# Inputs handed over with features on the partitions, and six PSUM banks for the first two column tiles

## The chip, the cores and the metric

The program runs on one core of a Trainium2 chip. The metric is the device time of one execution in microseconds (us). TensorE (PE; its weight loads are PEld), VectorE (DVE), ScalarE (ACT), GpSimd (POOL) and SyncE (SP) each run their own instructions in a fixed order; they wait for each other through semaphores. Nearly all DMAs are issued on SP's queue, and a DMA that waits holds up every DMA behind it in that queue.

## The reference

One layer of a decoder over 1024 prompt tokens and 8 sample requests of 4 tokens (1056 tokens), in float32:

```
x = x + mixer(rmsnorm(x, g_mix)) @ w_out       # retention (4 heads) and HGRN2 (4 heads), one projection w_in
x = x + cross_attn(rmsnorm(x, g_xa))           # 256 memory tokens, 4 heads of 256
x = x + swiglu(rmsnorm(x, g_ffn))
y = rmsnorm(x, g_final)
mem_k, mem_v = rmsnorm(mem, g_mem) @ w_xk, rmsnorm(mem, g_mem) @ w_xv    # prompt memory, both are outputs
rmsnorm(x, g) = x * rsqrt(mean(x*x, -1) + 1e-6) * g
```

The prompt attends to `mem_k` and `mem_v`; the sample requests attend to cached keys and values, `cache_mem_k[0, b, m, h, d]` for request b, memory token m, head h. Outputs are y, the recurrent states and the prompt's memory keys and values.

## The kernel before

**Layout.** Activations lie with features on the partitions: 8 tiles of 128 features, 1056 tokens wide, in three column blocks `GS` of 384, 384 and 288 tokens. Every float32 product is made of three matmuls (helper `mms`, line 220): both operands are split into a high part (a copy, on ACT, L195) and a low part (the difference, on POOL or DVE, L196 for weights), and high*high, high*low and low*high are summed in PSUM.

**Items.** A weight matrix is worked in column tiles of 128 features, each an `Item`. `run` takes an item: for every token block, 24 matmuls (8 feature tiles by three) into one PSUM bank, then an evacuation (`evac`). During an item the next item's weights are split (`w_split`), and at its end the weights of the item three on are loaded (`w_raw`, two DMAs of 256 KB into four `wraw` buffers). After each half of an item `tick` lets the generators in `sides` do one step each; all side work (recurrences, attention, loads) enters the instruction order that way. PSUM has eight banks: `mm` 2, `sm` 3, `o` 2, `u` 1.

**Start.** Tokens arrive with tokens on the partitions (`load_x`, nine tiles `xt`). `x_unit(g, k)` brings feature tile k of token block g to features first: PE transposes of up to three 128-token tiles (L789), ACT writes the high part scaled by the gain (L790), ACT or DVE writes the raw copy `xraw` (L792, L794), DVE the low part (L795). 24 units are worked in block order `GO` = (2, 0, 1), three units ahead of the matmuls of the first two items: the first HGRN2 head's query (item 0) and forget gate (item 1). `x_squares` (L799 on ACT, L801 on DVE) sums the squares of a token tile, `rstd_small` takes them to a power on POOL (L315), and `x_bcast` spreads the factors over the partitions with PE (L319, bank `u`) and a DVE copy into `rbc` (L809). An evacuation multiplies a bank by `rbc`, so it needs the block's factors; the two `mm` banks are used again for each block. The raw copies are stored to DRAM (`xT_d`) and come back as the residual. Gains come as rows and are transposed (L755). Item 2 (the value) follows under `run`.

**Later places.** `mem_load` brings the memory tokens in and transposes them (L913), inside the second retention head. `kv_proj_item` makes the memory keys (8 items, then 8 for the values); a side step transposes each result back to tokens first (L955), ACT copies it (L957) and SP stores it (L965). `sample_keys` loads the cached keys (`kb`, L1090), transposes them (32 steps of four, L1103) and ACT copies them to `keyT` (L1105), eight ahead of their use in `sample_attend`. These steps lie in the output projection (`c_items`, from the fifth on) and in the query projection of the cross attention.

Of the kernel before, what the change touches and what calls it, by code (L numbers as in the profile page):

```python
# [44 lines left out]
VB = 4  # L45
KLEAD = 2
PAUSES = {1: 2, 8: 2, 9: 2, 14: 0, 15: 0, 16: 0, 17: 0}
# [9 lines left out]
class Item:  # L57


    def __init__(self, src, kt, xs, evac, cols=GS, start=None, end=None, l_eng="pool", k0=0):  # L60
        self.src, self.kt, self.xs, self.evac, self.cols = src, kt, xs, evac, cols
        self.start, self.end, self.l_eng, self.k0 = start, end, l_eng, k0
        self.ks = range(kt)
        self.pieces = 2
        self.wide = False
        self.steps = None
        self.side_by_side = 3
        self.banks = None
        self.dst = None
        self.same = None  # L70
        self.split = None
        self.before_last = None

    def prepare(self, n):
# [18 lines left out]
def build(tc, ctx, a, outs):  # L93
# [29 lines left out]
    def ub():  # L123
        return psum("u", 1)
# [135 lines left out]
    def run(items):  # L260

        for it in items:
# [92 lines left out]

    xT_d = dr.tile([KT, P, T], F32, name="xT_d")
    x1_d = dr.tile([KT, P, T], F32, name="x1_d")
# [384 lines left out]

    gts = [hw.tile([n, P], F32, name="gt", tag="on", bufs=2) for n in (16, 32)]

    def load_gain(n):
        r0, r = gcol[n]
        src = a[n] if n == "hg_lb" else a[n][0:1]
        gt, r0 = (gts[0], r0) if r0 < 16 else (gts[1], r0 - 16)
        act.dma_start(gt[r0:r0 + r], src.rearrange("l (h p) -> (l h) p", p=P))

    def put_gains(i):
        n, lo = (16, 0), (32, 16)
        n, lo = (n, lo)[i]
        g_ps = ub()
        pe.transpose(g_ps[:, 0:n], gts[i], ident[:n, :n])  # L755
        dve.tensor_copy(gains[:, lo:lo + n], g_ps[:, 0:n])

    GO = (2, 0, 1)
    act.dma_start(ident, a["c_ident"])
    load_x(6)  # L760
    for n in ("g_mix", "hg_lb"):
        load_gain(n)
    load_x(7)
    load_x(8)
    w_raw()
    for i in (0, 1, 2):
        load_x(i)
    w_raw()
    for i in (3, 4, 5):
        load_x(i)  # L770
    dve.memset(ones, 1.0)
# [5 lines left out]

    xraw = [act_tile(k) for k in range(KT)]
    ss = tp.tile([P, 16], F32, name="ss", tag="ss", bufs=1)
# [3 lines left out]
    def x_unit(g, k):  # L783
        c = GS[g]
        w = width(g)
        pt = (sm if k % 2 else ob)()[:, :w]
        for i, rows in tiles_of(g):
            lo = i * P - c.start
            pe.transpose(pt[:, lo:lo + rows], xt[i][:rows, k * P:(k + 1) * P], ident[:rows, :rows])  # L789
        act.activation(X["h"][k][:, c], pt, AF.Copy, scale=gain("g_mix", k))  # L790
        if k % 2:
            act.activation(xraw[k][:, c], pt, AF.Copy)  # L792
        else:
            dve.tensor_copy(xraw[k][:, c], pt)  # L794
        dve.scalar_tensor_tensor(X["l"][k][:, c], pt, gain("g_mix", k), X["h"][k][:, c].bitcast(F32), op0=ALU.mult, op1=ALU.subtract)  # L795

# [25 lines left out]

    put_gains(0)
    xunits = [(g, k) for g in GO for k in range(KT)]
    AHEAD = 3
    for u in xunits[:AHEAD]:
        x_unit(*u)
        if u == xunits[0]:
            w_split()
    for n in ("g_xa", "g_mem", "g_ffn", "ret_gain", "hg_gain"):  # L830
        load_gain(n)
    first = mix_items[:2]
    w_first = []
    for it in first:
        it.start()
    banks = None

    def first_mms(j, g, k):
        mms(banks[j], pairs_of(first[j], w_first[j], GS[g], (k,)), first=(k == 0), last=(k == KT - 1))

    for n_, (g, k) in enumerate(xunits):
        if n_ + AHEAD < len(xunits):
            x_unit(*xunits[n_ + AHEAD])
        if k == 0:
            banks = [mm()[:, :width(g)] for _ in first]
        if n_ == 0:
            w_first.append(splits.pop(0))
        first_mms(0, g, k)
# [7 lines left out]
        if k == 5:  # L856
            x_bcast(g)
        if n_ == 2:
            lower_bound()
        if n_ == 4:  # L860
            act.activation(lw[:, 0, 0:1], ones[:, 0:1], AF.Sigmoid)
        if k == 3 and g != GO[-1]:
            for i, rows in tiles_of(GO[GO.index(g) + 1]):
                x_squares(i, rows)
        if n_ == 1:
            for i, rows in tiles_of(g):
                x_squares(i, rows)
        if n_ == KT - 1:
            put_gains(1)
        if k == KT - 1:  # L870
            first[0].evac(banks[0], g)
            if g == GO[-1]:
                w_split()
                for k_ in range(KT):
                    first_mms(1, g, k_)
            first[1].evac(banks[1], g)
        if n_ == KT:
            w_raw()
            w_raw()
            for t, n in ((lmask, "c_lmask"), (bsel, "c_bsel")):  # L880
                sp.dma_start(t, a[n])
    w_raw()
    done[0] = 2
    for k in (4, 5, 6, 7, 0, 1, 2, 3):
        sp.dma_start(xT_d[k], xraw[k])
    rope += [btile(0), btile(1)]
# [13 lines left out]
    def mem_load():  # L900
# [3 lines left out]
        mss = tp.tile([P, 4], F32, name="mss", bufs=1)  # L904
        for c in range(2):
            for i in range(2):
# [5 lines left out]
                for k in range(4):  # L912
                    pe.transpose(pt[:, k * P:(k + 1) * P], mtok[:, k * P:(k + 1) * P], ident)  # L913
                dve.tensor_copy(mT[c][:, :, i * P:(i + 1) * P], pt.rearrange("p (k t) -> p k t", k=4))
                act.activation(mtok, mtok, AF.Square, accum_out=mss[:, 2 * c + i:2 * c + i + 1])
                yield
# [26 lines left out]
    def kv_proj_item(wname, m, is_k, l_eng):  # L943
        def ev(pt, g):
            if is_k:
                t32 = k32(m)
            else:
                t32 = tmp("sg")[:, :NMEM]
            dve.tensor_tensor(t32, pt, kvs["rbm"][:, :NMEM], op=ALU.mult)

            def rest():
# [6 lines left out]
                ms = slice(m * P, (m + 1) * P)  # L958
                if not is_k:
                    for i in range(2):  # L960
                        act.activation(kvs["vh"][i][:, ms], tt[:, i * P:(i + 1) * P], AF.Copy)
                        dve.tensor_tensor(kvs["vl"][i][:, ms], tt[:, i * P:(i + 1) * P], kvs["vh"][i][:, ms].bitcast(F32), op=ALU.subtract)
                out = mk_o if is_k else mv_o
                yield
                sp.dma_start(out[0, 0].rearrange("(i p) h d -> p i (h d)", p=P)[:, :, ms], st.rearrange("p (i e) -> p i e", i=2))  # L965

# [64 lines left out]

    run(mix_items[2:4])
    for h in range(1, NH):
# [23 lines left out]
    def split_heads():  # L1057
        for i in range(6):
            yield
        for k in ORD[:6]:  # L1060
# [3 lines left out]
            yield  # L1064
            reload(k, xT_d, st_c)
            yield
# [16 lines left out]
    def sample_keys():  # L1083

        kbs = {}

        def load(n):
            if n < NH * NB:
                kbs[n] = kv.tile([P, 2, NMEM], F32, name="kb", bufs=KLEAD + 1)
                sp.dma_start(kbs[n], a["cache_mem_k"][0, n % NB, :, n // NB].rearrange("(i p) d -> p i d", p=P))  # L1090

        for n in range(KLEAD):
            load(n)
            yield
        for n in range(NH * NB):
            while kstate["made"] - kstate["used"] >= KTB:
                yield
            load(n + KLEAD)
            pt = sm()
            kb = kbs.pop(n)  # L1100
            for e_ in range(2):
                for i in range(2):
# [15 lines left out]
    nothing = lambda: None  # L1118
    c_items[0].stepwise(ORD, [nothing] * 6 + [lambda k=k: split_o(k) for k in ORD[6:]] + [lambda k=k: reload(k, xT_d, st_c) for k in ORD[6:]])
    c_items[-1].ks = ORD  # L1120
# [762 lines left out]
    for n_, (c, tiles) in enumerate(FG):  # L1883
# [22 lines left out]
        else:  # L1906
# [10 lines left out]
        'w_up', 'w_down', 'g_final']  # L1917
_OUTS = [(1, 1024, 1024), (8, 4, 1024), (1, 1, 4, 128, 128), (1, 1, 4, 128, 128), (1, 1, 256, 4, 256), (1, 1, 256, 4, 256),
         (1, 8, 4, 128, 128), (1, 8, 4, 128, 128)]
# [36 lines left out]


# [16 lines left out]
```

## Time and profile before

| | |
|---|---|
| median of 3 runs | 1737.16 us (1736.64 to 1738.53) |
| the profiled execution, its own time | 1737.18 us |
| its span, first to last instruction | 1735.4 us |
| PE busy | 1683.4 us, 97% of the span |
| DVE, ACT, POOL busy | 855.6, 567.6, 595.1 us |
| DMA moved | 154.83 MB, 89 GB/s on average |

The rows below read as follows. A timeline row gives start, duration, engine, line, operation, result and operands with their tile names, shape and count, and in brackets the idle time of the engine before it with what ended that. Successive matmuls overlap, so the distance between two starts is the time that one takes from its engine. A chain row is a piece of the chain of work that ended last. A row of a table by stretches gives the busy time of each engine in the stretch (with instruction counts), then the granted TensorE clock, the busy share of the DMA engines, and GB/s.

### The profile page before, as it was taken

What the parts mean: (1) busy time and instruction counts of PE and PEld (TensorE: products, weight loads), DVE (VectorE), ACT (ScalarE), POOL (GpSimd) and SP (SyncE); (2) the same over time, 40 slices, a digit from 0 to 9 for tenths busy, and PEclk for the clock granted to TensorE, in tenths of its full rate; (3) what the DMA queues carried; (4) which work ended last, traced back from release to release, by engine and by line L of the source; (5) the groups of instructions that cost most, each with busy time, mean ns of one, the idle gap of its engine ahead of it and who ended that gap; (6) DMA issues with size and microseconds to landing.
All of it is one profiled execution on the core that took longest, in us unless ns stands there. A gap on an engine that the chain in (4) does not pass through costs nothing.

```text
span 1735.4 us, 33455 instructions
## 1 busy us (share of the span) xinstructions
PE 1683.4 (97%) x13752; PEld 1616.6 (93%) x13752; DVE 855.6 (49%) x1625; ACT 567.6 (33%) x1162; POOL 595.1 (34%) x511
## 2 busy tenths in 40 slices
PE   7999999999999999999999889999999999999997
PEld 6999889899999899999989889999999999999987
DVE  6365565532336511422246986665565666322335
ACT  5221222232225522344444452223322223221213
POOL 2222223433543543200032235555555552222211
PEclk9999999999999999999999999999999999999999
DMA  4511211122215734133243212222222224332112
GB/s 153 181 40 50 64 38 52 41 85 62 63 31 148 232 115 158 51 122 116 92 130 87 73 31 75 75 83 93 90 75 81 75 75 138 99 101 90 59 46 101
DMA packets 206968, 154.83 MB, mean 89 GB/s; under 512 B 8784, under 2 KB 191904, under 8 KB 206816
## 3 DMA queue, kind: packets, MB, share of 16 engines
q1 hardware_dynamic: 206576, 152.61, 28.3%
q8 instruction: 108, 1.77, 0.4%
q14 instruction: 44, 0.36, 0.1%
q10 hardware_dynamic: 240, 0.09, 0.0%
HBM read 122.06 MB, written 30.61 MB: 88 GB/s over the span
## 4 chain that ended last, share of the span: by engine, by line
PE 83%; DVE 6%; issue 4%; ACT 3%; DMA 2%; POOL 2%; SPq 0%; ACTq 0%; POOLq 0%; DVEq 0%
PE mm L220 52%; PE o L220 12%; PE sm L220 7%; PE sm L1158 1%; PE sm L532 1%; PE u L422 1%; PE sm L1103 1%; PE o L435 1%; PE u L220 1%; PE sm L403 1%; PE o L437 1%; ACT wh L195 1%; POOL xl L305 1%; POOL wl L196 1%; DMA wraw<-in_w_xo_dram 1%
## 5 line engine op out<-in xcount | busy, mean ns | idle before, releaser
L220 PE MATMUL mm<-xh,wh 128*128 128x384 f32 (+3 forms) x1756 | 565.9, 329 | 5.3 <-DVE z L674 1.9
L220 PE MATMUL mm<-xl,wh 128*128 128x384 f32 (+3 forms) x1756 | 544.9, 317 | 0.8 <-DVE xl L305 0.5
L220 PE MATMUL mm<-xh,wl 128*128 128x384 f32 (+4 forms) x1692 | 537.8, 318 | 2.9 <-POOL wl L196 2.9
L196 POOL TENSOR_TENSOR wl<-wraw,wh 128x512 fp32r<-128x512 f32 (+2 forms) x155 | 191.4, 1250 | 518.3 <-ACT wh L195 399.7
L220 PEld LDWEIGHTS mm<-xh,wh 128*128 128x128 f32 x1756 | 328.1, 189 | 20.5 <-issue 14.2
L220 PEld LDWEIGHTS mm<-xl,wh 128*128 128x128 f32 x1756 | 328.5, 190 | 2.4 <-DVE xl L305 0.9
L220 PEld LDWEIGHTS mm<-xh,wl 128*128 128x128 f32 x1692 | 320.0, 189 | 4.3 <-POOL wl L196 3.8
L195 ACT ACTIVATE wh<-wraw 128x512 fp32r<-128x512 f32 (+2 forms) x266 | 153.8, 600 | 316.6 <-PE mm L220 136.1
L196 DVE TENSOR_TENSOR wl<-wraw,wh 128x512 fp32r<-128x512 f32 (+1 forms) x111 | 112.1, 1014 | 34.7 <-ACT wh L195 31.8
L220 PE MATMUL o<-xl,wh 128*128 128x264 f32 (+2 forms) x444 | 127.8, 288 | 0.2
L220 PE MATMUL o<-xh,wh 128*128 128x264 f32 (+2 forms) x444 | 127.8, 288 | 0.0
L220 PE MATMUL o<-xh,wl 128*128 128x264 f32 (+2 forms) x444 | 127.4, 287 | 0.0
L220 PE MATMUL mm<-n,wh 128*128 128x264 f32 (+2 forms) x586 | 123.9, 302 | 3.2 <-ACT n L195 1.6
L1588 POOL TENSOR_TENSOR sil<-sil,rbc 128x528 f32<-128x528 f32 x44 | 63.2, 1456 | 137.9 <-ACT sil L1587 137.9
L220 PEld LDWEIGHTS mm<-n,wh 128*128 128x128 f32 x586 | 95.5, 188 | 4.1 <-ACT n L195 1.9
L1752 DVE TENSOR_TENSOR a<-mm,a 128x384 f32<-128x384 f32 (+1 forms) x71 | 37.3, 525 | 122.7 <-PE mm L220 122.6
L195 ACT ACTIVATE wh<-sum 128x512 fp32r<-128x512 f32 x88 | 55.3, 629 | 115.3 <-PE o L220 69.0
L220 PE MATMUL mm<-n,wl 128*128 128x264 f32 (+2 forms) x293 | 88.3, 302 | 0.7 <-POOL wl L196 0.7
L220 PEld LDWEIGHTS o<-xl,wh 128*128 128x128 f32 x444 | 84.0, 189 | 0.9 <-POOL xl L305 0.8
L220 PEld LDWEIGHTS o<-xh,wh 128*128 128x128 f32 x444 | 84.0, 189 | 0.0
L220 PEld LDWEIGHTS o<-xh,wl 128*128 128x128 f32 x444 | 83.6, 188 | 0.0
L315 POOL TENSOR_TENSOR orr<-rs,nhalf 128x4 f32<-128x4 f32 (+3 forms) x33 | 27.7, 840 | 139.7 <-DVE rs L314 129.9
(450 smaller groups left out, 3147.4 us busy)
## 6 DMA issues: line engine op xcount, KB each, us to landing
wraw<-in_w_in_dram SPq DMA_DIRECT2D x64, 256.0 KB, 2.9
wraw<-in_w_gate_dram SPq DMA_DIRECT2D x44, 256.0 KB, 2.9
wraw<-in_w_up_dram SPq DMA_DIRECT2D x44, 256.0 KB, 2.9
p_d<-sil SPq DMA_DIRECT2D x40, 264.0 KB, 3.5
vb<-in_cache_mem_v_dram SPq DMA_DIRECT2D x32, 256.0 KB, 3.9
kb<-in_cache_mem_k_dram SPq DMA_DIRECT2D x32, 256.0 KB, 2.7
wraw<-in_w_down_dram SPq DMA_DIRECT2D x32, 256.0 KB, 2.8
wraw<-in_w_xo_dram SPq DMA_DIRECT2D x23, 256.0 KB, 4.1
```

The source lines that it names most:

```text
L195: act.activation(h_, src, AF.Copy)
L196: e.tensor_tensor(l_, src, h_.bitcast(F32), op=ALU.subtract)
L220: pe.matmul(out, l_, r_, start=(first and i == 0), stop=(last and i == n - 1), **kw)
L305: e.tensor_tensor(xl[:, cc], src[:, cc], xh[:, cc].bitcast(F32), op=ALU.subtract)
L315: pool.tensor_tensor(out, t[:rows, :n], nhalf[:rows, :n], op=ALU.pow)
L403: pe.transpose(pt[:, c * P:(c + 1) * P], src[:, lo:lo + P], ident)
L422: pe.matmul(u[:, c * P:(c + 1) * P], ktok[:, cc * P:(cc + 1) * P], vtok[:, cc * P:(cc + 1) * P], start=True, stop=True)
L435: pe.matmul(dst, att[:, cc * P:(cc + 1) * P], vtok[:, cc * P:(cc + 1) * P], start=True, stop=(cc == 0))
L437: pe.matmul(dst, q[:, cc * P:(cc + 1) * P], S[:, cc - 1], start=False, stop=True)
L532: pe.matmul(pt[32 * j:32 * j + 32, c * w:(c + 1) * w], kk[:, lo:lo + 32], t_, start=True, stop=True)
L1588: pool.tensor_tensor(both, both, r[:, c2_], op=ALU.mult)
L1752: dve.tensor_tensor(x2[m][:, GS[g]], pt, x2[m][:, GS[g]], op=ALU.add)
```

## The change

- The host hands over the tokens also features first (`x_T`), the gains as columns (`c_gains`), the sample's keys features first, 2 KB per partition (`cache_mem_k`), and the memory tokens features first (`c_memT`); the prompt's memory keys are written features first and turned by the host.
- `x_unit` becomes two instructions, high and low part, out of a loaded tile; its transposes, raw copy and bank are gone. Tokens in token order are still loaded, for the squares, behind `x_T` of their block. `xT_d` and its eight stores are gone; the residual is read from `x_T`.
- The first item's weights and the gains come on ACT's queue; its two low parts are both made on DVE.
- The first two items use six banks, two for each token block (`mm`, `o`, `sm`). Squares, broadcast and evacuation move back: block 2's squares to the 12th unit and its evacuation behind the 16th; block 0's squares behind both items; block 0's evacuation, block 1's squares and block 1's evacuation into `first_rest`, a side generator that runs in item 2, which takes its blocks in the order `GO`.
- The transposes of memory tokens, of memory keys (with their ACT copy) and of the sample's keys (with theirs) are gone; DMAs write `mT` and `keyT`, and the key result is stored by SP in the evacuation itself.

```diff
@@ -268,9 +268,9 @@
-                for g in range(len(it.cols)):
-                    group(it, w, g, g == 0)
-                    if g == 1:
+                for n_, g in enumerate(it.order or range(len(it.cols))):
+                    group(it, w, g, n_ == 0)
+                    if n_ == 1:
                         w_raw()
@@ -740,34 +739,27 @@
+    act.dma_start(gains, a["c_gains"])
+    first = mix_items[:2]
+    raws[0] = [wtile("wraw", KH, F32) for _ in range(2)]
+    for t, ks in zip(raws[0], halves(KT)):
+        act.dma_start(t, first[0].src[ks.start * P:ks.stop * P].rearrange("(k p) m -> p k m", p=P))
...
     act.dma_start(ident, a["c_ident"])
...
+    load_T(2, range(4))
+    load_T(2, range(4, KT))
     w_raw()
-    for i in (0, 1, 2):
+    load_T(0, range(KT))
+    for i in (6, 7, 8):
         load_x(i)
...
+    load_T(1, range(KT))
@@ -775,24 +767,14 @@
     def x_unit(g, k):
-        c = GS[g]
-        w = width(g)
-        pt = (sm if k % 2 else ob)()[:, :w]
-        for i, rows in tiles_of(g):
-            lo = i * P - c.start
-            pe.transpose(pt[:, lo:lo + rows], xt[i][:rows, k * P:(k + 1) * P], ident[:rows, :rows])
-        act.activation(X["h"][k][:, c], pt, AF.Copy, scale=gain("g_mix", k))
-        if k % 2:
-            act.activation(xraw[k][:, c], pt, AF.Copy)
-        else:
-            dve.tensor_copy(xraw[k][:, c], pt)
-        dve.scalar_tensor_tensor(X["l"][k][:, c], pt, gain("g_mix", k), X["h"][k][:, c].bitcast(F32), op0=ALU.mult, op1=ALU.subtract)
+        x, h_, l_ = (t[k][:, GS[g]] for t in (xraw, X["h"], X["l"]))
+        act.activation(h_, x, AF.Copy, scale=gain("g_mix", k))
+        dve.scalar_tensor_tensor(l_, x, gain("g_mix", k), h_.bitcast(F32), op0=ALU.mult, op1=ALU.subtract)
@@ -820,31 +802,37 @@
+    banks = {g: [f()[:, :width(g)] for _ in first] for g, f in zip(GO, (mm, ob, sm))}
...
+        if n_ == 11:
+            squares(GO[0])
+        if n_ == 15:
+            first_evac(GO[0])
+    w_split()
+    for k_ in range(KT):
+        first_mms(1, GO[-1], k_)
+    squares(GO[1])
...
+    def first_rest():
+        first_evac(GO[1])
+        squares(GO[2])
+        yield
+        first_evac(GO[2])
+
+    mix_items[2].order = GO
+    side(first_rest())
+    run(mix_items[2:3])
@@ -947,6 +932,9 @@
             dve.tensor_tensor(t32, pt, kvs["rbm"][:, :NMEM], op=ALU.mult)
+            if is_k:
+                sp.dma_start(mk_o[m], t32)
+                return
@@ -1082,27 +1068,11 @@
-            load(n + KLEAD)
-            pt = sm()
-            kb = kbs.pop(n)
-            for e_ in range(2):
-                for i in range(2):
-                    pe.transpose(pt[:, (2 * e_ + i) * P:(2 * e_ + i + 1) * P], kb[:, i, e_ * P:(e_ + 1) * P], ident)
             keyT[n] = kv.tile([P, 2, NMEM], F32, name="keyT", bufs=KTB)
-            act.activation(keyT[n], pt.rearrange("p (e m) -> p e m", e=2), AF.Copy)
+            sp.dma_start(keyT[n], a["cache_mem_k"][n // NB, n % NB])
```

How the instruction order moves, at three places.

DVE, at the end of the start, before: the squares (`s`, `ss`) of block 1 stand between the low parts (`xl`) of the last units, ahead of the broadcast copy (`rbc`) of block 0.

```order
L314 TENSOR_SCALAR rs<-ss 128x1
L801 SCALAR_TENSOR_TENSOR s_162,ss<-b_121 128x1024
L314 TENSOR_SCALAR rs<-ss 128x1 x2
L795 SCALAR_TENSOR_TENSOR xl_116<-sm,gains,xh_108 128x384
L794 COPY a_151<-o 128x384
L795 SCALAR_TENSOR_TENSOR xl_109<-o,gains,xh_101 128x384
L809 COPY rbc<-u 128x384
```

The same squares now, on DVE, in item 2: between the two last broadcast copies stand an evacuation of block 0 (items 0 and 1, out of the `o` banks) and the squares, then the value's first evacuation (`V`).

```order
L791 COPY rbc<-u 128x384
L673 TENSOR_TENSOR z<-o,rbc 128x384
L683 TENSOR_TENSOR z<-o,rbc 128x384
L685 TENSOR_SCALAR b_193<-sg,oml,lower 128x384
L686 TENSOR_SCALAR b_192<-b_193 128x384
L314 TENSOR_SCALAR rs<-ss 128x1
L783 SCALAR_TENSOR_TENSOR s_176,ss<-b_120 128x1024
L314 TENSOR_SCALAR rs<-ss 128x1 x2
L660 TENSOR_TENSOR V<-mm,rbc 128x288
L791 COPY rbc<-u 128x384
```

What moved: block 1's squares went from ahead of block 0's broadcast to behind its evacuation, and its own broadcast follows them directly. On PE the two broadcasts (L319) stand 12 matmuls of 288 columns apart.

SP, in the memory keys, before: each key store (`out_4`, out of ACT's copy `z`) and the weight loads after it.

```order
L178 DMA wraw_6110<-in_w_xk_dram 128x4x128
L178 DMA wraw_6112<-in_w_xk_dram 128x4x128
L1052 DMA a4_6160<-xT_d_91 128x1056
L965 DMA out_4_dram<-z_6165 128x2x128
L178 DMA wraw_6186<-in_w_xk_dram 128x4x128
L178 DMA wraw_6188<-in_w_xk_dram 128x4x128
```

And now:

```order
L936 DMA out_4_dram<-b0_5867 128x256
L178 DMA wraw_5966<-in_w_xk_dram 128x4x128
L178 DMA wraw_5968<-in_w_xk_dram 128x4x128
L1038 DMA a4_6016<-in_x_T_dram 128x1056
L936 DMA out_4_dram<-b0_5867 128x256
```

What moved: the store of key tile m stood behind the weight loads issued at the end of item m, and waited for a copy made inside item m+1; it now stands ahead of those loads and waits for the evacuation of item m.

PE, in the fifth tile of the output projection, before: the first of the 32 steps that transpose the sample's keys.

```order
L220 MATMUL mm_7427<-xl3_7015,wh_7291 128x384
L220 MATMUL mm_7427<-xh3_7014,wl_7292 128x384
L1103 MATMUL sm_7442<-ident_83,kb_7407 128x128 x4
L220 MATMUL mm_7427<-xh4_6086,wh_7295 128x384
L220 MATMUL mm_7427<-xl4_6087,wh_7295 128x384
```

And now:

```order
L220 MATMUL mm_7242<-xh3_6829,wh_7106 128x384
L220 MATMUL mm_7242<-xl3_6830,wh_7106 128x384
L220 MATMUL mm_7242<-xh3_6829,wl_7107 128x384
L220 MATMUL mm_7242<-xh4_5941,wh_7110 128x384
L220 MATMUL mm_7242<-xl4_5942,wh_7110 128x384
```

What moved: the four transposes are gone, as at the other 31 steps; apart from removed transposes and the start up to item 2, PE's order is the same in both kernels.

## Rows read from the trace of the kernel before

**Rows 1.** The page: PE's busy time, and the engines' shares of the chain that ended last.

```profile
PE 1683.4 (97%) x13752; PEld 1616.6 (93%) x13752; DVE 855.6 (49%) x1625; ACT 567.6 (33%) x1162; POOL 595.1 (34%) x511
...
PE 83%; DVE 6%; issue 4%; ACT 3%; DMA 2%; POOL 2%; SPq 0%; ACTq 0%; POOLq 0%; DVEq 0%
```

**Rows 2.** The instructions of line 1103, the transposes of the sample's keys: durations (ns, least, median, most), first and last start (us).

```profile
L1103 PE MATMUL sm<-ident,kb x128: 270/272/474, 655.3 to 847.3; 128*128 128x128 f32 x128
```

**Rows 3.** The chain in the output projection, where the key transposes begin (start, us, engine, tile, line).

```profile
650.18 5.02 DMA kb<-in_cache_mem_k_dram
...
655.25 1.11 PE sm L1103 x4
656.37 3.17 PE mm L220 x12
659.54 0.44 PE sm L1103 x4
...
671.64 2.10 PE mm L220 x12
```

**Rows 4.** The timeline of PE there: the first key transposes with the wait ahead of them, and two matmuls of 384 columns behind.

```profile
655.25 1.11 PE L1103 MATMUL sm<-ident,kb 128*128 128x128 f32 x4 [2.19 <-DMA kb<-in_cache_mem_k_dram]
...
656.80 0.52 PE L220 MATMUL mm<-xh,wl 128*128 128x384 f32 x1
657.12 0.52 PE L220 MATMUL mm<-xh,wh 128*128 128x384 f32 x1
```

**Rows 5.** Busy time by stretches around that place, and (last row) in the query projection of the cross attention.

```profile
654.00:656.00 2.00, 0.75 (x4) 0.75 (x5) 0.00 (x0) 0.00 (x0) 0.00 (x0) 0.79 0.70 245
656.00:658.00 2.00, 2.00 (x8) 2.00 (x7) 0.00 (x0) 0.60 (x1) 0.00 (x0) 0.50 0.22 61
...
740.00:750.00 10.00, 10.00 (x75) 8.80 (x75) 3.04 (x7) 6.35 (x17) 0.00 (x0) 1.00 0.49 153
```

**Rows 6.** The start by stretches: to the first projection matmul; to where both items have five feature tiles of block 2; to the end of items 0 and 1; to the end of item 2.

```profile
0.00:10.35 10.35, 3.62 (x13) 2.04 (x13) 2.05 (x6) 3.96 (x8) 1.48 (x5) 1.00 0.83 265
10.35:22.91 12.56, 11.98 (x44) 9.62 (x44) 11.72 (x32) 8.16 (x18) 5.12 (x5) 1.00 0.95 299
22.91:52.74 29.83, 27.98 (x182) 26.67 (x181) 22.51 (x45) 17.14 (x35) 7.86 (x10) 1.00 0.02 5
52.74:64.44 11.70, 11.70 (x74) 11.70 (x73) 2.65 (x6) 2.20 (x4) 3.44 (x3) 1.00 0.96 367
```

**Rows 7.** The timeline of PE in the start: the wait for item 1's low weights, and matmuls of 288 columns early and later.

```profile
19.62 0.61 PE L220 MATMUL mm<-xh,wl 128*128 128x288 f32 x1 [0.51 <-POOL wl L196]
...
20.50 0.44 PE L220 MATMUL mm<-xh,wl 128*128 128x288 f32 x1
20.75 0.44 PE L220 MATMUL mm<-xh,wh 128*128 128x288 f32 x1
...
24.02 0.29 PE L220 MATMUL mm<-xh,wh 128*128 128x288 f32 x1
24.16 0.29 PE L220 MATMUL mm<-xl,wh 128*128 128x288 f32 x1
```

**Rows 8.** DMA issues of the first 60 us: tile, count, size of each, median us from issue to landing.

```profile
wraw<-in_w_in_dram SPq DMA_DIRECT2D x10, 256.0 KB, 5.7
...
vtok<-in_x_prompt_dram SPq DMA_DIRECT2D x1, 512.0 KB, 4.1
```

**Rows 9.** Low parts of weights on DVE over the whole run: count, durations (ns, least, median, most).

```profile
L196 DVE TENSOR_TENSOR wl<-wraw,wh x111: 416/693/1815, 9.5 to 1467.1; 128x512 fp32r<-128x512 f32 x109, 128x256 fp32r<-128x256 f32 x2
```

**Rows 10.** The timeline of ACT, DVE and POOL in the start, for durations: a square on ACT and on DVE, three factors on POOL, a low part, the broadcast copy, a first product, a sigmoid, two high parts of weights, a gate.

```profile
12.54 1.05 ACT L799 ACTIVATE S<-ktok 128x1024 f32<-128x1024 f32 x1
13.48 1.21 DVE L801 SCALAR_TENSOR_TENSOR s<-vtok 128x1024 f32<-128x1024 f32 x1
21.60 2.61 POOL L315 TENSOR_TENSOR rr<-rs,nhalf 128x1 f32<-128x1 f32 x3 [2.03 <-DVE rs L314]
47.28 0.61 DVE L795 SCALAR_TENSOR_TENSOR xl<-sm,gains,xh 128x384 fp32r<-128x384 f32 x1
47.81 0.55 DVE L809 COPY rbc<-u 128x384 f32<-128x384 f32 x1
48.87 0.56 DVE L674 TENSOR_TENSOR z<-mm,rbc 128x384 f32<-128x384 f32 x1 [0.51 <-PE mm L220]
49.46 0.53 ACT L675 ACTIVATE sg<-z 128x384 f32<-128x384 f32 x1 [2.57 <-DVE z L674]
49.89 1.14 ACT L195 ACTIVATE wh<-wraw 128x512 fp32r<-128x512 f32 x2
54.24 0.48 DVE L686 TENSOR_SCALAR b<-sg,oml,lower 128x384 f32<-128x384 f32 x1 [0.66 <-ACT sg L685]
```

**Rows 11.** The instructions of lines 913 and 955, the transposes of memory tokens and of memory keys: durations (ns, least, median, most), first and last start (us).

```profile
L913 PE MATMUL sm<-ident,lmask x16: 272/273/273, 355.1 to 381.9; 128*128 128x128 f32 x16
...
L955 PE MATMUL sm<-ident,b x16: 271/272/328, 545.1 to 572.0; 128*128 128x128 f32 x16
```

**Rows 12.** The timeline at the end of the memory keys: SP's issue of weights, POOL's low part of the same weights, and PE's first use of that low part.

```profile
570.14 1.12 SPq L178 DMA_DIRECT2D wraw<-in_w_xv_dram  x2
...
575.61 1.30 POOL L196 TENSOR_TENSOR wl<-wraw,wh 128x512 fp32r<-128x512 f32 x1 [2.04 <-ACT wh L195]
...
576.96 0.39 PE L220 MATMUL mm<-xh,wl 128*128 128x256 f32 x1
```

More of the change, by code (lines that the diff above doesn't have):

```diff
@@ L72, in __init__ @@
         self.before_last = None
+        self.order = None
     def prepare(self, n):
@@ L821, in lower_bound, with squares, first_evac @@
         dve.tensor_scalar(oml, lower, -1.0, 1.0, op0=ALU.mult, op1=ALU.add)
-    put_gains(0)
     xunits = [(g, k) for g in GO for k in range(KT)]
     AHEAD = 3
-    for u in xunits[:AHEAD]:
-        x_unit(*u)
[L828 to L833, printed above, removed]
+    splits[0] = first[0].split = ([], [])
+    wstate["split"] = 1
+    for u, raw in zip(xunits[:2], raws.pop(0)):
+        h_, l_ = wtile("wh", KH), wtile("wl", KH)
+        split2(h_, l_, raw, dve)
+        splits[0][0].append(h_)
+        splits[0][1].append(l_)
+        x_unit(*u)
+    x_unit(*xunits[2])
+    w_first = [splits.pop(0)]
     for it in first:
         it.start()
-    banks = None
+    banks = {g: [f()[:, :width(g)] for _ in first] for g, f in zip(GO, (mm, ob, sm))}
     def first_mms(j, g, k):
-        mms(banks[j], pairs_of(first[j], w_first[j], GS[g], (k,)), first=(k == 0), last=(k == KT - 1))
+        mms(banks[g][j], pairs_of(first[j], w_first[j], GS[g], (k,)), first=(k == 0), last=(k == KT - 1))
+    def squares(g):
+        for i, rows in tiles_of(g):
+            x_squares(i, rows)
+    def first_evac(g):
+        x_bcast(g)
+        for it, bank in zip(first, banks[g]):
+            it.evac(bank, g)
     for n_, (g, k) in enumerate(xunits):
@@ L855, in build @@
                 first_mms(1, g, k_)
-        if k == 5:
-            x_bcast(g)
         if n_ == 2:
             lower_bound()
-        if n_ == 4:
+        if n_ == 6:
             act.activation(lw[:, 0, 0:1], ones[:, 0:1], AF.Sigmoid)
[L862 to L876, printed above, removed]
         if n_ == KT:
             w_raw()
+            for i in range(6):
+                load_x(i)
             w_raw()
@@ L1064, in split_heads @@
             yield
-            reload(k, xT_d, st_c)
+            reload(k, a["x_T"], st_c)
             yield
@@ L1083, in sample_keys @@
     def sample_keys():
[L1085 to L1094, printed above, removed]
         for n in range(NH * NB):
@@ L1118, in build @@
     nothing = lambda: None
-    c_items[0].stepwise(ORD, [nothing] * 6 + [lambda k=k: split_o(k) for k in ORD[6:]] + [lambda k=k: reload(k, xT_d, st_c) for k in ORD[6:]])
+    c_items[0].stepwise(ORD, [nothing] * 6 + [lambda k=k: split_o(k) for k in ORD[6:]] + [lambda k=k: reload(k, a["x_T"], st_c) for k in ORD[6:]])
     c_items[-1].ks = ORD
@@ L1955, in shape_constants, with laid_out @@
     return c
+def laid_out(inputs):
+    data = {n: np.ascontiguousarray(inputs[n]) for n in _INS if n[:2] != "g_" and n[-5:] != "_gain" or n == "g_final"}
+    keys = np.asarray(inputs["cache_mem_k"])[0].transpose(2, 0, 3, 1).reshape(NH, NB, 2, P, NMEM)
+    data["cache_mem_k"] = np.ascontiguousarray(keys.transpose(0, 1, 3, 2, 4))
+    rows = [np.asarray(inputs[n]).reshape(-1, P) for n in ("g_mix", "hg_lb", "g_xa", "g_mem", "g_ffn", "ret_gain", "hg_gain")]
+    data["c_gains"] = np.ascontiguousarray(np.pad(np.concatenate(rows).T, ((0, 0), (0, 48 - sum(len(r) for r in rows)))))
+    tokens = np.concatenate([np.asarray(inputs[n]).reshape(-1, D) for n in ("x_prompt", "x_sample")])
+    data["x_T"] = np.ascontiguousarray(tokens.T.reshape(KT, P, T))
+    data["c_memT"] = np.ascontiguousarray(np.asarray(inputs["mem_prompt"])[0].T.reshape(2, 4, P, NMEM).transpose(0, 2, 1, 3))
+    return data
 def kernel(**inputs):
@@ L1963 @@
     arrays, aps = {}, {}
-    data = {n: np.ascontiguousarray(inputs[n]) for n in _INS}
+    data = laid_out(inputs)
     data.update(shape_constants())
```

58 lines of the change are left out of this document (15 added, 43 removed).

## The prediction

> **What bounds the kernel now.** I read the page first: PE is busy 97% of the span and makes up 83% of the chain that ended last [rows 1]. So one instruction taken out of PE's order is worth its whole time wherever PE runs without a gap, and nothing where PE waits at that place anyway. Next I read the places that the change touches, one by one: the key transposes in the chain and the timeline [rows 2 to 5], the start by stretches [rows 6], where PE is busy but its matmuls stand at twice the later distance [rows 7], and last the memory tokens and keys. All sums are made against the profiled execution, 1737.18 us, which is within 0.02 us of the median.
>
> **The sample's keys: 17.6 us off.** 32 steps of four transposes go [rows 2]. A step stands in the chain with 0.44 us [rows 3], and in the query projection, where they lie densest, PE is busy 10.00 of 10 us [rows 5]: nothing hides them. 31 x 0.44 = 13.6. The first step runs from 655.25 to the next matmul, 0.8 us, at half pace. Ahead of it PE waits 2.19 us for `kb` [rows 4]; the chain shows that DMA, 5.02 us, as the releaser [rows 3]. Behind it 12 matmuls take 3.17 us where 12 later ones take 2.10 [rows 3]: the granted clock falls to 0.79 in the stretch of the wait and 0.50 in the next [rows 5], the level of 1.2 GHz, and matmuls of 384 columns stand 0.32 us apart [rows 4] instead of 2.10/12 = 0.175. That is 1.07. Sum 13.6 + 0.8 + 2.2 + 1.07 = 17.6. ACT's 32 copies go too, but ACT isn't on the path there. The new key loads need only a free `keyT`, which `sample_attend` releases eight requests ahead of use, so I cost them at nothing on PE; their cover is those eight slots, and if it fails PE waits for a load, up to the 5.02 us of [rows 3] once. Bounds: 13.5 (the wait, its slow matmuls and the half-pace part come back elsewhere) to 18.5.
>
> First what the trace shows: after 2.19 us without work PE ran at the lower level. The Trainium skill, "TensorE: Matmul & The Clock Gate", section "Why this matters for your kernels", warns of PE-idle gaps between bursts of matmuls because the clock goes back to half; by that rule the change, which takes this gap away and makes a new one in item 2 (below), gains 1.07 here and loses some 1.7 there, which is what the rows give as well.
>
> **The start, to the end of item 2: 6.3 us off (2 to 11).** Item 2 now ends at 64.44 [rows 6]. I rebuild it with the new orders.
> - First matmul. Before, the gains, nine PE transposes and the split stand ahead of it, at 10.35 [rows 6]. Now only the gains, item 0's weights and `x_T` are needed. A 512 KB load issued at 0.74 landed 4.1 us later, a weight load of 256 KB takes 5.7 in the median [rows 8]: usable at 5.0 to 7, I take 5.0, since this load is early in its queue. ACT's high part (0.57) and a DVE low part (0.69, [rows 9]) follow: first matmul about 6.1.
> - Block 2. DVE makes both weight low parts and the first units' `xl` (0.5 each) and paces PE to 8.25, five units of item 0 are done at 10.9. Item 1's weights, behind eight token loads on SP, are split at 12.05 (ACT, two in 1.14, [rows 10]) and 13.35 (POOL, 1.28 a low part). 13 matmuls at 0.24 [rows 7] end at 16.45, the point that before is reached at 22.91: 6.5 earlier. I keep the half pace, since before the 0.24 spacing lasts to about 4 us behind the last wait at 19.62 [rows 7].
> - Blocks 0 and 1 of items 0 and 1. Each unit loses three PE transposes. 4 x 0.24 + 14 x 0.133 + 48 x 0.175 give 27.65 at the end of block 0; block 2's broadcast 0.7; item 0's 24 matmuls in two parts with a wait of 1.55 between (unit 20's low part stands behind block 2's evacuation on DVE: copy 0.45, two products, two gates and the `xl`, some 0.5 each [rows 10]); item 1's 24 x 0.175. End at 38.35, before 52.74: 14.4 earlier.
> - Item 2, blocks 2 and 0. 12 x 0.133, block 0's broadcast (its factors are ready by about 39.5, no wait), 12 x 0.133: 42.2. Then PE stands before the second broadcast. Behind it is DVE's row in the order: the copy of block 0, two products, two gates, the squares; on ACT two sigmoids and two squares of 1.05 + 0.19; on POOL the factors, 2.61/3 = 0.87 each [rows 10]. From the first broadcast's end: 0.55 + 2 x 0.56 + 0.53 + 1.24 + 1.21 + 0.35 + 2 x 0.83 = 6.6, so the factors come at 47.2 and **PE idles 5.0 us**. Queued behind on PE are item 2's last 48 matmuls, which need none of these factors. Then 0.7 + 48 x 0.175 = 56.3, and as at 654 the clock should fall: there the half pace lasted from 655.25 to about 658.4 [rows 3, 4], and half of that time, 1.6, is lost; I take 1.8 for the longer wait. End 58.1 against 64.44.
>
> The tokens cost nothing in this sum. 10.2 MB of inputs (twice 4.33 MB of tokens, six weight loads of 256 KB) must land by about 42 us; the stretches of the start moved 265 to 367 GB/s where loads were queued [rows 6], which takes 38 us at the lowest rate. The bounds 2 and 11: no early start of the weights and a longer wait in item 2 (8), against no wait there.
>
> **Memory tokens: 1.75 us off.** 16 transposes in four groups of four, 4 x 0.44, in a dense stretch [rows 11]. Both bounds within 0.3.
>
> **Memory keys: 1.0 us off (-1.5 to 2.1).** 16 transposes, eight pairs [rows 11], at 0.11 each from half of an 0.44 step of four, are 1.8 to 2.1 us. What is added: SP's store of item m now waits for that item's evacuation and stands ahead of the next weight loads, where before it waited for a copy of the item before. Queued behind are the weight loads, then ACT, POOL and PE. That path is just in time: the load issued at 570.14 feeds a low part at 575.61 to 576.91, which PE uses at 576.96 [rows 12]. An evacuation's 0.56 [rows 10] and one issue of 0.5 in a few items takes back some half.
>
> **Sum.** 17.6 + 6.3 + 1.75 + 1.0 = 26.6, so 1737.18 - 26.6 = 1710.5. Gains put in as columns, the removed stores of `xT_d` and ACT's lost copies are off the path; their DMA moved beside PE at full pace.
>
> **Rivals.**
> - *A, the clock rises earlier, or does not fall at item 2's wait:* 1.8 us more, 1708.7. For it: with no transposes the early matmuls are all full ones. Against: the half pace in [rows 4] after a shorter wait. In the start the granted-clock column reads 1.00 [rows 6] although the spacing is that of the lower level [rows 7], so rows don't decide it. The Trainium skill, "TensorE: Matmul & The Clock Gate", section "Part 4: PE-mode transpose", holds that transposes don't count as PE work for the clock; by that rule the rise comes earlier here. Chance 0.12.
> - *B, weights later through the memory keys:* eight items each lose the store's wait, eight times some 0.5 instead of the gain of 1.0: 1710.5 + 4 = 1714.5. For it: the just-in-time path of [rows 12]; against: one item in view only. Chance 0.10.
> - *C, the attention's own latency takes the place of the key steps:* the steps stand between scores and probabilities of the sample attention; if 24 of the 32 only filled such waits, 24 x 0.44 = 10.5 is lost: 1721. Against: PE without any gap in [rows 5]. Chance 0.10.
> - *D, six banks don't do what they say:* the wait moves from a block's end to item 2 and is 8 us more than the 5 that I put, or the first weights come as late as before: 1718. Chance 0.08.
> - *E, slower than before:* the start becomes bound by its loads, since x is loaded twice. The rows of [rows 6] give 265 to 299 GB/s; 10.2 MB would have to come below some 140 GB/s, 73 us in place of 42, to lose more than the 27 that the rest gains. Reads of 1152 or 1536 bytes a row might be slower than token rows of 4 KB; a factor of two is unlikely. Past 1741. Chance 0.02.
>
> **How the numbers follow.** The forecast has 0.58, and A to E the chances above. The range is 1702 to 1720: it holds the forecast with its bounds (the keys' 13.5, the start's 2 to 11; all low bounds at once are unlikely), A, B and D, and leaves C and E out. A gain below 0.2%, 3.5 us, is about what a measurement of this kernel can't tell from no change; only E with a mild rate or C with D come there: same 0.03, slower 0.02, faster 0.95.
>
> **What would show it.** In the profile of the changed kernel: no line of key transposes and no wait or clock below 1.00 near 650 to 660; the query projection still without gaps (else C); items 0 and 1 ending near 38 and item 2 near 58, with one wait of about 5 us before its second broadcast and a shorter one in unit 20 of the start; first matmul near 6; in the memory keys, whether PE waits for `wl` more than before (B). If item 2 ends past 62, the start's step is wrong (D or E); if it ends before 55, the wait for block 1's factors is.

## The result: slower, where 27 us less was forecast

| | before | changed |
|---|---|---|
| median (4 runs each) | 1737.65 us (1736.64 to 1738.53) | 1757.81 us (1755.62 to 1758.81) |
| ratio to before | 1 | 1.0114, 95% interval 1.0097 to 1.0132 |
| the profiled execution, its own time | 1737.18 us | 1758.38 us |
| its span | 1735.4 us | 1756.4 us |

The changed kernel is 20 us slower; the forecast of 1710.5 us and its range of 1702 to 1720 were wrong. The page of the changed kernel answers to [rows 1]: PE is busy 6.6 us less, in a longer span; its share of the chain falls from 83% to 80%, and DMA's rises from 2% to 4%.

```profile
PE 1676.8 (95%) x13518; PEld 1605.7 (91%) x13518; DVE 841.1 (48%) x1608; ACT 545.2 (31%) x1110; POOL 593.6 (34%) x510
...
PE 80%; DVE 6%; issue 5%; DMA 4%; ACT 3%; POOL 2%; SPq 0%; POOLq 0%; ACTq 0%; DVEq 0%
```

Where the time went is read by following the first or last start of one and the same line in both traces (the view of a line):

| place | before | changed | moved since the place above |
|---|---|---|---|
| first evacuation of the item behind item 2 | 68.9 | 60.5 | -8.4 |
| first evacuation of a memory key | 542.4 | 533.5 | -0.5 |
| first evacuation of the output projection | 611.0 | 644.2 | **+42.1** |
| last evacuation of the cross attention's query | 874.6 | 889.3 | -18.5 |
| first scaled tile for the layer behind the cross attention (DVE, line 1384 before) | 936.3 | 956.0 | +5.0 |
| last instructions on the output (DVE, line 1862 before) | 1730.5 | 1751.4 | +1.2 |

So the start and the sample's keys gave what the prediction wanted of them. Sixteen items in between, the memory keys and values, lost more than both. PE's waits in the changed kernel (total us, times, longest) name it; in the kernel before, the first of these isn't in the list, and the second stands with 3.6 us:

```profile
PE mm L220 <- ACT wh L195: 15.8, 13, 3.2
PE mm L220 <- POOL wl L196: 11.8, 15, 0.9
PE mm L220 <- ACT xh L776: 6.4, 2, 6.2
PE u L319 <- POOL rr L315: 5.3, 2, 3.6
PE sm L943 <- DVE sg L934: 5.1, 7, 3.5
```

PE waits for split weights. The evacuations of memory keys (tile `b`) and values (tile `sg`), first and last start, give the time of an item: (586.0 - 533.5)/7 = 7.50 us for a key and 5.40 for a value, where the kernel before (line 949) took 4.03 and 3.63.

```profile
L949 DVE TENSOR_TENSOR b<-mm,rbc x8: 409/422/425, 542.4 to 570.6; 128x256 f32<-128x256 f32 x8
L949 DVE TENSOR_TENSOR sg<-mm,rbc x8: 411/414/414, 574.0 to 599.4; 128x256 f32<-128x256 f32 x8
...
L934 DVE TENSOR_TENSOR b<-mm,rbc x8: 409/417/424, 533.5 to 586.0; 128x256 f32<-128x256 f32 x8
L934 DVE TENSOR_TENSOR sg<-mm,rbc x8: 414/415/417, 592.4 to 630.2; 128x256 f32<-128x256 f32 x8
```

The chain that ended last, followed through one memory key, shows what an item waits for (L936 is the store of the key, L178 the load of weights). The four rows behind the chain are from the timelines of PE, DVE and SP: the last matmul of the next item, its evacuation, its store and the load behind that.

```profile
542.03 0.34 DVE b L934
...
542.38 0.36 SPq L936
...
542.79 0.43 SPq L178
...
543.26 3.36 DMA wraw<-in_w_xk_dram
...
546.73 0.64 ACT wh L195
...
547.39 1.01 DVE wl L196
548.40 0.60 DVE on L450
549.00 0.60 DVE oss L444
...
549.63 0.24 DVE rs L314
...
543.89 0.28 PE L220 MATMUL mm<-xl,wl 128*128 128x256 f32 x1
...
549.77 0.42 DVE L934 TENSOR_TENSOR b<-mm,rbc 128x256 f32<-128x256 f32 x1
...
550.21 0.36 SPq L936 DMA_DIRECT2D out_dram<-b  x1
550.68 0.97 SPq L178 DMA_DIRECT2D wraw<-in_w_xk_dram  x2
```

It is a closed loop: an evacuation releases the key store on SP; behind the store SP issues the next weights; they land, ACT and DVE split them; and DVE reaches the next evacuation (549.77) only behind that split, because `w_split` stands ahead of `evac` in the program. PE had ended the matmuls of that next item at 544.2, so its bank stood ready for 5.6 us. SP then issues the next load at 550.68, 7.9 us after the last. One item's load is in flight at a time. In [rows 12] the load issued at 570.14 had 6.8 us until PE used it, while the loads of other items went on beside it.

The stretches show what this does: the whole of the sixteen items, before and changed; one piece of them in the changed kernel, with the granted clock at 0.54; then the ten microseconds in which the first of the sample's keys are loaded (683.4), which answer to [rows 5], now without a gap.

```profile
542.40:611.00 68.60, 65.04 (x536) 62.38 (x537) 40.24 (x80) 34.68 (x72) 35.79 (x27) 1.00 0.76 225
533.50:644.20 110.70, 82.76 (x519) 73.39 (x520) 37.42 (x79) 33.91 (x66) 35.19 (x28) 0.85 0.49 145
...
560.00:570.00 10.00, 7.82 (x54) 5.66 (x55) 2.33 (x4) 3.51 (x6) 2.54 (x2) 0.54 0.50 155
...
680.00:690.00 10.00, 10.00 (x62) 10.00 (x62) 1.57 (x3) 2.54 (x5) 4.61 (x5) 1.00 0.86 289
```

The 42.1 us have two parts. PE stands idle for 27.9 us of the sixteen items (110.70 - 82.76) where it stood idle for 3.6 before, 24.4 us more; and it is busy 17.7 us longer with fewer instructions, at a granted clock of 0.85 in place of 1.00.

### The profile page after: what moved, and what is told of

Same layout as the page of the kernel before. It is cut to its first block, busy times and chain, and to the rows that moved or that the text cites. A ratio compares the mean times of both kernels' runs of the same rounds, so it can differ in the third digit from the quotient of the medians.

```text
span 1756.4 us, 32900 instructions
## 1 busy us (share of the span) xinstructions
PE 1676.8 (95%) x13518; PEld 1605.7 (91%) x13518; DVE 841.1 (48%) x1608; ACT 545.2 (31%) x1110; POOL 593.6 (34%) x510
## 3 DMA queue, kind: packets, MB, share of 16 engines
q8 instruction: 106, 1.74, 0.4%
## 4 chain that ended last, share of the span: by engine, by line
PE 80%; DVE 6%; issue 5%; DMA 4%; ACT 3%; POOL 2%; SPq 0%; POOLq 0%; ACTq 0%; DVEq 0%
PE mm L220 50%; PE o L220 12%; PE sm L220 7%; DMA wraw<-in_w_xv_dram 1%; PE sm L1128 1%; ACT wh L195 1%; DMA wraw<-in_w_xk_dram 1%; PE sm L531 1%; PE sm L402 1%; PE u L421 1%; PE u L220 1%; PE o L434 1%; DMA wraw<-in_w_xo_dram 1%; PE o L436 1%; POOL wl L196 1%
## 5 line engine op out<-in xcount | busy, mean ns | idle before, releaser
L220 PE MATMUL mm<-xh,wh 128*128 128x384 f32 (+3 forms) x1724 | 557.2, 330 | 24.4 <-ACT wh L195 15.8
L220 PE MATMUL mm<-xh,wl 128*128 128x384 f32 (+3 forms) x1660 | 530.4, 319 | 11.3 <-POOL wl L196 11.3
L220 PE MATMUL mm<-xl,wh 128*128 128x384 f32 (+3 forms) x1724 | 539.0, 320 | 1.0 <-DVE xl L305 0.5
L220 PEld LDWEIGHTS mm<-xh,wh 128*128 128x128 f32 x1724 | 325.3, 192 | 42.1 <-ACT wh L195 19.0
L196 DVE TENSOR_TENSOR wl<-wraw,wh 128x512 fp32r<-128x512 f32 x112 | 109.6, 983 | 90.1 <-ACT wh L195 87.5
L220 PE MATMUL o<-xl,wh 128*128 128x264 f32 (+1 forms) x460 | 133.9, 291 | 0.2
L220 PE MATMUL o<-xh,wh 128*128 128x264 f32 (+1 forms) x460 | 133.9, 291 | 0.0
L220 PE MATMUL o<-xh,wl 128*128 128x264 f32 (+1 forms) x460 | 133.5, 290 | 0.0
L220 PEld LDWEIGHTS o<-xl,wh 128*128 128x128 f32 x460 | 87.8, 191 | 0.8 <-POOL xl L305 0.8
L220 PEld LDWEIGHTS o<-xh,wh 128*128 128x128 f32 x460 | 87.7, 191 | 0.0
L220 PEld LDWEIGHTS o<-xh,wl 128*128 128x128 f32 x460 | 87.3, 190 | 0.0
```

Source lines behind the costliest of these rows:

```text
L196: e.tensor_tensor(l_, src, h_.bitcast(F32), op=ALU.subtract)
L220: pe.matmul(out, l_, r_, start=(first and i == 0), stop=(last and i == n - 1), **kw)
```

## The experiments

**What had been passed over.** The change takes out one call: behind the loop of the start the kernel before had a call of `w_raw()`, the fifth item's load in the program; the changed one has none there and only four loads in the start. The full diff has this as one removed line, which the core of the diff above leaves out. With it gone, every later load in the program stands one item later: the load for item j at the end of item j-2, no more of item j-3 (a lead of two items in place of three). Theory 1: what counts is how many items lie between the item that a load on SP's queue is for and the item whose result the store ahead of it waits for. Theory 2: it is only the key store, now released by the evacuation.

Four kernels separate them. On the changed kernel: one load more (e1), the store later (e2), and both (e3). On the old kernel: the call taken out (e4). The edits of e1, e2 and e4:

```diff
     w_split()
+    w_raw()
     for k_ in range(KT):
```

```diff
             if is_k:
-                sp.dma_start(mk_o[m], t32)
+                def store():
+                    yield
+                    yield
+                    sp.dma_start(mk_o[m], t32)
+
+                side(store())
                 return
```

```diff
                 sp.dma_start(t, a[n])
-    w_raw()
     done[0] = 2
```

e1, expected: 

> The changed kernel with one weight load more behind the start (the old kernel's fifth call of w_raw), so that the load for item j stands again at the end of item j-3 and not of item j-2. Theory 1 (distance in SP's queue: a load stands behind a store that waits for the result of an earlier item; the changed kernel let the load of item j wait for the result of item j-2, one load in flight): memory keys and values lose nearly nothing any more, about 35 to 42 us come back, total 1712 to 1722. Theory 2 (the key store's wait for the evacuation alone, whatever the distance): only little comes back, the keys stay at about 8 us an item, total above 1745.

e2, expected: 

> The changed kernel with the key store of item m put on SP's queue at the end of item m+1, where the old kernel had it; no load more. Theory 1: the keys come back (some 20 to 24 us, since their loads then wait for the result three items back), the values stay slow, as their stores and loads are untouched: total 1733 to 1740. Theory 2: keys and values come back, about 40 us: total 1712 to 1722.

e3, expected: 

> Both: one load more behind the start, and the key store at the end of the next item. Theory 1: the distance is four items for the keys, PE waits for weights there hardly at all; total 1708 to 1716, up to 4 us below the kernel with the load alone. Theory 2: as the kernel with the later store alone.

e4, expected: 

> The old kernel with its fifth call of w_raw taken out and nothing else: the load of item j stands at the end of item j-2. Theory 1: memory keys and values go to about 5.3 to 6 us an item from 3.6 to 3.9, 16 items, so 25 to 35 us slower: 1763 to 1778. Theory 2: the store's place is the old one, so no change: 1735 to 1741.

Measured, with the time of an item from the evacuations in each profile as above, and the sixteen items from the first evacuation of a memory key to the first of the output projection:

| kernel | median us | ratio to before, 95% interval | us a key, a value | sixteen items, us |
|---|---|---|---|---|
| before | 1737.65; 1737.42 beside e1 to e4 | 1 | 4.03, 3.63 | 68.6 |
| changed | 1757.81 | 1.0114 (1.0097 to 1.0132) | 7.50, 5.40 | 110.7 |
| e1, load back | 1715.38 | 0.9870 (0.9855 to 0.9884) | 4.14, 3.89 | 71.8 |
| e2, store later | 1732.19 | 0.9959 (0.9945 to 0.9973) | 3.97, 5.31 | 83.2 |
| e3, both | 1711.30 | 0.9849 (0.9832 to 0.9865) | 4.17, 3.57 | 69.2 |
| e4, old kernel without the call | 1767.45 | 1.0166 (1.0151 to 1.0181) | 5.57, 5.40 | 95.1 |

All four came out as theory 1 said (e2 0.8 us below the time expected), and theory 2 falls with e1 and e4: the old kernel with its store in the old place loses 30 us by that one line. In the SP queue of e4, two values' rows show the shorter form of the loop, store of ACT's copy `z`, then weights, 5.5 us apart:

```profile
591.35 0.38 SPq L964 DMA_DIRECT2D out_dram<-z  x1
591.83 1.01 SPq L178 DMA_DIRECT2D wraw<-in_w_xv_dram  x2
596.86 0.38 SPq L964 DMA_DIRECT2D out_dram<-z  x1
597.35 1.01 SPq L178 DMA_DIRECT2D wraw<-in_w_xv_dram  x2
```

The two causes don't simply add up. Moving the store costs 27.5 us with the short lead (110.7 against 83.2) and 2.6 with the long one (71.8 against 69.2). The stretch of e1 stands at the old kernel's clock and rate again:

```profile
535.50:607.30 71.80, 64.52 (x520) 61.04 (x521) 39.98 (x80) 32.32 (x64) 35.11 (x28) 1.00 0.77 223
```

The 5.0 us lost up to 956.0 hang on the call too: the same stretch loses 4.1 in e4 and 0.4 in e1.

**The stores on another queue (e6).** The changed kernel, lead unchanged:

```diff
-                sp.dma_start(mk_o[m], t32)
+                act.dma_start(mk_o[m], t32)
...
-                sp.dma_start(mv_o[0, 0]...
+                act.dma_start(mv_o[0, 0]...
```

Expected: 

> The changed kernel with the stores of memory keys and values on ACT's queue in place of SP's; the loads keep their later place (item j at the end of item j-2). Theory 1 in its strict form (it is only what stands ahead of a load in SP's queue that holds it, the place of the call in the program by itself does nothing): keys and values come back, 1712 to 1722, with some 4 us of the cross attention's output projection still lost. If the later place of the load costs by itself, also without a waiting store ahead: above 1735.

Measured: 1725.96 us, ratio 0.9920 (0.9898 to 0.9942), between the two times expected. With no store ahead, the values come back (3.70 us an item), the keys only in part (5.41), and the sixteen items take 79.5 us. So the late call isn't harmless by itself, but most of the loss goes with the stores: 31 of the 42 us. SP's rows show another waiting DMA among the loads, the reload of the residual (line 1038), once 10.6 us behind the load before it:

```profile
556.51 0.92 SPq L178 DMA_DIRECT2D wraw<-in_w_xv_dram  x2
567.15 0.34 SPq L1038 DMA_DIRECT2D a<-in_x_T_dram  x1
568.83 0.92 SPq L178 DMA_DIRECT2D wraw<-in_w_xv_dram  x2
```

That these reloads hold the remaining 11 us is read from the trace; no run tested it.

**The terms alone.** The old kernel with only the keys changed (e5; the loop of `sample_keys` as in the diff above), and with only the start changed (e9: the kernel of e1 with the old memory tokens, memory keys and sample's keys).

e5, expected: 

> The old kernel with one part of the change alone: the sample's keys come features first, their 32 transpose steps, ACT copies and the two-step load are gone. If the term of the prediction holds, 17 to 19 us off the old kernel: 1718 to 1721, and no wait or clock fall near 655. If the attention's own latency had taken the steps' place (rival C), some 7: 1730.

e9, expected: 

> The start of the changed kernel alone (x features first, six banks), with the old kernel's lead of three items and its memory tokens, memory keys and sample keys. The prediction's term of the start was 6.3 us; in the runs so far the end of item 2 came 4.9 to 8.4 us earlier, by the moment at which the matmuls go from 0.24 to 0.13 us apart (13.6 to 19.1 us): 1729 to 1733.

Measured: e5 1725.15 us, ratio 0.9919 (0.9891 to 0.9948), 9 to 19 us off; its runs lay from 1719.41 to 1729.86, so the median fell between the two times expected and decides nothing. In its profiled run, 1721.44 us, the last evacuation of the query comes 18.5 us earlier, of which 2.8 are lost again by the end. The places agree with the forecast and not with rival C. e9 1733.72 us, 0.7 above the span expected; ratio 0.9954 (0.9937 to 0.9970), 5 to 11 us off.

**The wait in item 2 (e7, e8, each run in two series).** On e3, the broadcast for block 1 goes two ticks later (e7); e8 has ACT's queue for the stores as well:

```diff
         squares(GO[2])
         yield
+        yield
+        yield
         first_evac(GO[2])
```

e7, expected: 

> The kernel with both repairs (one load more, key store one item later), and block 1's broadcast and evacuation two ticks later in item 2, so that 48 matmuls stand between the two broadcasts in place of 12. The 3.6 us for which PE waits there go, and the clock doesn't fall behind them: 4 to 6 us below the kernel with both repairs, 1705 to 1708. If the wait was only moved (the last block of the value then waits for its factors), no change: 1710 to 1712.

e8, expected: 

> The same, and the stores of memory keys and values on ACT's queue. If waits in SP's queue are what still makes PE wait for weights there (4.2 us in all in the kernel with both repairs), 1 to 4 us less than the kernel with the later broadcast: 1702 to 1706. If those waits are the DMAs' own time (both stages move over 200 GB/s), no change.

Second series, e3 again: 

> The kernel with both repairs again, beside the next two on one chip: 1709 to 1713.

e7 again: 

> With the later broadcast: if the wait and the slow matmuls behind it are gone for good, 4 to 6 us below the kernel with both repairs; if the difference seen before was only the moment at which the clock rises in the start, none.

e8 again: 

> With the stores on ACT's queue too: 0 to 2 us below the kernel with the later broadcast.

In the first column e3 stands in the series of e1 to e4 and on another chip than e7 and e8; the second column is one series on one chip.

| kernel | first series | second series |
|---|---|---|
| e3 | 1711.30, 0.9849 (0.9832 to 0.9865) | 1712.04, 0.9833 (0.9809 to 0.9858) |
| e7 | 1709.56, 0.9821 (0.9797 to 0.9844) | 1708.56, 0.9809 (0.9782 to 0.9836) |
| e8 | 1706.77, 0.9817 (0.9797 to 0.9837) | 1706.63, 0.9803 (0.9776 to 0.9830) |

The wait is gone from the profile: the stretch in e7's second run, and below it the same in e3's, with a granted clock of 0.83 in the stretch of the 3.63 us of waiting.

```profile
40.00:50.00 10.00, 10.00 (x61) 9.81 (x60) 7.70 (x16) 4.75 (x9) 6.23 (x7) 1.00 0.62 192
```

```profile
40.00:50.00 10.00, 6.34 (x31) 5.80 (x30) 6.82 (x15) 4.22 (x8) 5.89 (x7) 0.83 0.62 190
```

The medians put e7 1.7 and 3.5 us below e3, and e8 2.8 and 1.9 below e7, but the intervals overlap: in the medians the order is likely and its size is not settled, and the 4 to 6 us expected of e7 were not reached there. At its own place the gain does show. The first evacuation of the item behind item 2 stands at 55.3 and 54.7 us in e7's two profiles and at 54.7 and 57.2 in e8's, against 60.4 to 60.9 and 63.0 to 64.0 in kernels with the wait (two groups, see the last section): 5.1 to 6.8 us. What covers it is scatter elsewhere: e7's ten runs go from 1702.28 us at a mean granted clock of 0.996 to 1712.62 at 0.988. That e8's other queue gains anything over e7 is not shown. e8 beats both kernels, by 1.6 to 2.2% against before.

## Why the prediction was wrong

- **Memory keys: the step that failed.** The prediction put 1.0 us off (-1.5 to 2.1) and its rival B 4 us on; measured were 42.1 on, keys and values together. It saw the store ahead of the weight loads and the "just in time" path, and priced an evacuation (0.56) and an issue (0.5) in a few items, or some 0.5 in eight items for B, as a delay that is added to the path behind the store: weight loads, then ACT, POOL and PE. That path left out DVE, on which it closes into a loop: the evacuation that releases the next store stands on DVE behind the split of the weights whose load the store before held back. And the prediction took the lead of three items as given, though the change removed the call that made it; so the memory values, for which it had no term at all, lost 1.8 us an item. With the call back (e1) the sixteen items take 3.2 us more than before, with the store later too (e3) 0.6 more in one run and 0.8 less in the other. B named the right place and a tenth of the price; its own sum also leaves out that the gain of 1.0 would go, which makes it 5 on, 1715.5.
- **The sample's keys: right.** 17.6 forecast, 18.5 in the changed kernel's trace. The wait and the fall of the clock went, as the row at 680 shows, and rival C didn't happen. By its median the term alone (e5) measures 9 to 19 us.
- **The start: right in mechanism; its size depends on when the early matmuls speed up.** 6.3 forecast, 8.4 in this run and 5 to 11 by e9. In this run the half pace ended at 13.6, earlier than the sum had it; in profiled runs where it lasted to 17.8 to 19.1, near the 17.4 of the sum, the start gave 5.0 to 5.9. The rows of PE that answer to [rows 7], each with its wait:

```profile
6.20 0.61 PE L220 MATMUL mm<-xh,wh 128*128 128x288 f32 x1 [6.20 <-ACT xh L776]
...
13.38 0.40 PE L220 MATMUL mm<-xh,wl 128*128 128x288 f32 x1 [0.89 <-POOL wl L196]
...
29.34 0.44 PE L220 MATMUL sm<-xh,wh 128*128 128x384 f32 x1 [0.62 <-ACT xh L776]
30.39 0.44 PE L220 MATMUL sm<-xl,wh 128*128 128x384 f32 x1 [0.61 <-DVE xl L777]
...
44.83 1.83 PE L319 MATMUL u<-ident,rr 128*128 128x128 f32 x6 [3.63 <-POOL rr L315]
```

  6.1 was forecast for the first, 13.35 for the second, 1.55 for the two waits in unit 20's place (1.23), 5.0 for the wait of the last (3.63). Behind that wait the clock fell as forecast: granted 0.83 from 40 to 50 us.
- **Memory tokens: right.** 1.75 forecast, 1.74 measured between two evacuations of `V` that enclose the sixteen transposes, before and changed:

```profile
342.81 0.56 DVE L661 TENSOR_TENSOR V<-mm,rbc 128x384 f32<-128x384 f32 x1 [0.93 <-PE mm L220]
401.35 0.56 DVE L661 TENSOR_TENSOR V<-mm,rbc 128x384 f32<-128x384 f32 x1 [1.70 <-PE mm L220]
...
335.66 0.56 DVE L660 TENSOR_TENSOR V<-mm,rbc 128x384 f32<-128x384 f32 x1 [0.90 <-PE mm L220]
392.46 0.56 DVE L660 TENSOR_TENSOR V<-mm,rbc 128x384 f32<-128x384 f32 x1 [1.70 <-PE mm L220]
```

  That is 58.54 us and 56.80. The four profiled kernels with the transposes (before, e4, e5, e9) all show 58.53 or 58.54, the ten profiled runs without them 56.80 or 56.81. Over the whole way from item 2 to the memory keys the traces move by -1.9 to +2.6 us from run to run, with and without that part; the rest comes mostly in steps of about 1.5 us at other waits, told in the last section.
- **The rivals.** The first half of A happened in this run: the early matmuls went to 0.13 us apart at 13.6, where the sum had them at half pace till 17.4; its second half, no fall at item 2's wait, did not. C, D and E did not happen: the kernel is slower, which only E had, but not by E's cause. DMA moved 13.37 MB in the first 45 us, 297 GB/s, and no wait of PE there was ended by a load directly.

With both repairs the kernel takes 1711.3 and 1712.0 us. That is within 2 us of the 1710.5 forecast, in part by luck. In the two profiles of e3 the start gives 5.9 and 8.0 (6.3 forecast), the memory tokens 1.7 (1.75), the sample's keys 18.6 and 18.5 (17.6), the memory keys and values 0.6 us more and 0.8 less than before (1.0 less); but their spans are 22.5 and 25.4 us below before's, not 26.6, since other places took some back. The single terms held for the change without its two slips in SP's queue; that the total came so near also needed losses and gains elsewhere to cancel.

## What to carry to other kernels

Count the lead of a prefetch again, in items, whenever a prologue is rewritten: one call left out at the start of this kernel cost nothing for 530 us and then some 40 (42 between the changed kernel and e1, 30 in the old kernel). When a store joins the queue that carries the loads, follow what it waits for back through that engine's own order; if it ends at the consumer of an earlier load on the same queue, the loads have become a loop, and its price is the whole way round, here 7.5 us an item in place of 4.0, and not the wait that the rows of before show.

## What the runs showed of the hardware

The moment at which the early matmuls of 288 columns go from 0.24 to 0.13 us apart fell in two groups, in kernels whose start is the same up to there: 13.4 to 14.1 us in six profiled runs (the changed kernel, e7 and all four of the last series) and 17.8 to 19.1 in five (e1, e2, e3, e6, e8). The first evacuation of the item behind item 2 then came 8.0 to 8.5 us earlier than before in the first group and 5.0 to 5.9 in the second (kernels with item 2's wait). One kernel, e3, is in the second group in its first run and in the first in its second, and e6, e7 and e8, on one chip, fall into both. Gaps of 0 to 1.7 us between the first two units differ from run to run as well, but e3's first run had none, so they alone don't decide. What does decide stays open. The granted-clock column reads 1.00 in both.

One and the same wait of PE lowers the clock in one run and not in another. In e7's first run (first two rows) and its second (last two) PE waits 1.68 us at the same instruction; in the first the clock stays at 1.00, in the second the matmuls of 384 columns soon behind it stand 0.32 us apart in place of 0.175:

```profile
168.41 0.69 PE L560 MATMUL sm<-Q,K 128*64 128x64 f32 x16 [1.68 <-DVE b L569]
165.00:175.00 10.00, 8.32 (x73) 7.56 (x73) 6.02 (x11) 3.20 (x9) 1.84 (x2) 1.00 0.37 105
...
167.76 0.69 PE L560 MATMUL sm<-Q,K 128*64 128x64 f32 x16 [1.68 <-DVE b L569]
165.00:175.00 10.00, 8.32 (x62) 7.50 (x61) 5.43 (x11) 2.57 (x7) 1.20 (x1) 0.83 0.37 105
```

Such a fall costs about 1.5 us here: the next evacuation of `V` comes that much later, counted from the item behind item 2. Between item 2 and the memory keys e7's second run has about 4.5 us more of such steps than its first, and e3's second 3.0 more than its first. Why a run falls into it is not shown.
